# The first projection's data brought k-tile by k-tile, x and weights in one transfer

## The chip, the cores and the metric

The kernel runs on one core of a Trainium2 chip. The metric is device time in microseconds, the median of several runs of the whole program.

## The reference

Three transformer layers on one sequence of 256 tokens with 1024 features, in float32. The change is at the very start of the first, which has two attentions side by side:

```python
proj = jnp.einsum('bsd,df->bsf', h, w_in)          # 1024 -> 1440
c_q, c_kv, k_r, q_s, k_s, v_s = _split_cols(proj, AB_SPLITS)
q = jnp.einsum('bsr,rf->bsf', _rms_norm(c_q, q_norm), w_uq)
kv = jnp.einsum('bsr,rf->bsf', _rms_norm(c_kv, kv_norm), w_ukv)
o_a = _mla_attention(q_nope, q_rope, kv[..., :MLA_NOPE], k_rope, kv[..., MLA_NOPE:])
o_b = _swa_sink_attention(q_s, k_s, v_s, sinks)     # 8 heads, window of chunks
x = _layer_norm(ALPHA * x + concat(o_a, o_b) @ w_out); x = _layer_norm(ALPHA * x + swiglu(x))
```

A second layer with two other attentions and a third block with gates, a spatial mixer and cross-attention follow. The first stage below computes 512 of the 1440 columns: `c_q` (384) and `v_s` (128).

## The kernel before

**Exact products in three passes.** Each float32 operand is split into a high part, rounded to the type fp32r on ACT (a copy), and a low part, the rest, subtracted on DVE. A product is then x high times w high, x high times w low, x low times w high (`gx`, lines 421 to 428), all accumulated in one PSUM bank. In `gx` x (128 tokens) is the stationary side and the weights are the moving side, 512 columns wide in the first stage.

**Weights** come from one packed stream in HBM in the order in which the kernel asks for them (`raw`, `block`, `w`, lines 383 to 415). `block` issues a transfer on SP's queue, the high part on ACT and the low part on DVE. Later weights go through five buffers with the tag `raw`; in the first stage they land in buffers with the tag `h`.

**The first stage** (`start`, line 608). Seven products of a zeroed tile run first. Then x transposed and the 512 columns of weights come in five groups of k-tiles (a k-tile is 128 of the 1024 features): 0, 1, 2-3, 4-5, 6-7, each as one transfer of weights and one of x. `mixer_ab` (lines 674 to 677) forms 48 products: eight k-tiles, two token halves (`p1`, two PSUM banks), three passes. Then the values are copied out and the sum of squares of `c_q` is formed (lines 683 to 686), and the next stage (288 columns, lines 688 to 691), the norms and their transposes (`norm_T`), the other projections and the eight heads of each attention follow.

**What sets the order.** All instructions are recorded by the class `Order` and put in order by a planner (`issue`, lines 191 to 336): a list scheduler that replays each engine with assumed costs, latencies and a transfer rate (lines 46 to 54) and takes, on each engine, the ready instruction that was written first. So a change at the start also changes the planned times of what follows, and with them the order on every engine, until the planned order falls back into the old one. All instructions are emitted on line 336, which is why the profile shows L336 for nearly everything; tiles tell them apart: `g` are PSUM banks of projections, `a` those of attention and transposes, `h` split operands, `L` softmax tiles, `s` small ones, `xT` the split x.

Of the kernel before, what the change touches and what calls it, by code (L numbers as in the profile page):

```python
# [10 lines left out]
F32 = mybir.dt.float32  # L11
F32R = mybir.dt.float32r
AF = mybir.ActivationFunctionType
OP = mybir.AluOpType
# [3 lines left out]
S = 256  # L18
KT = D // 128
# [18 lines left out]
def ar(a, n):  # L38
    return list(range(a, a + n))
# [299 lines left out]
class Net:  # L339
# [268 lines left out]
    def start(self):  # L608
        nc, one = self.nc, self.one
        T = lambda name, shape: one(shape, F32, name)  # L610
        xt, self.xT = self.new_xT()
        self.xt0 = xt
        self.w_first = []
        rows = self.kt(KT)
        cols = ar(0, 384) + ar(1312, 128)
        z = self.tmpp([128, 128], F32, tag="si")
        nc.vector.memset(z, 0.0)
        p = self.pa()
        for i in range(WARM):
            nc.tensor.matmul(p[:, 0:128], z, z, start=True, stop=True)  # L620
        w = []
        for k0, k1 in ((0, 1), (1, 2), (2, 4), (4, 6), (6, 8)):
            w += self.w("ab_w_in", 0, rows[k0:k1], cols, self.hp)
            self.block(("xT", 0, rows[k0:k1], None), k1 - k0, S, out=(xt[:, 0, k0:k1, :], xt[:, 1, k0:k1, :]), pool=self.hp)
        self.g1 = w
        self.ident = T("ident", [128, 128])
        nc.sync.dma_start(self.ident, self.a["ident"], early=True)
        self.mhalf = T("mhalf", [128, 1])
        nc.gpsimd.memset(self.mhalf, -0.5)
        self.res = T("res", [128, 2, D])  # L630
# [38 lines left out]
    def mixer_ab(self):  # L669
        nc, V, A = self.nc, self.nc.vector, self.nc.scalar  # L670
        a, xT = self.a, self.xT
        rows = self.kt(KT)

        p1 = [self.pg(), self.pg()]
        for k in range(KT):
            for t in range(2):
                self.gx(p1[t], self.tok(xT[k:k + 1], t), self.g1[k:k + 1], k == 0, k == KT - 1)
        gq = self.gbp([128, 640], F32, tag="gb")
        self.bcast("ab_q_norm", 384, tile_=gq[:, 0:384])
        self.bcast("ab_kv_norm", 256, tile_=gq[:, 384:640])  # L680
# [7 lines left out]
        w = self.w("ab_w_in", 0, rows, ar(384, 288))  # L688
# [15 lines left out]
        w = self.w("ab_w_in", 0, rows, ar(1184, 128))  # L704
# [4 lines left out]
        for j in (0, 2):  # L709
            w = self.w("ab_w_in", 0, rows, [c for i in (j, j + 1) for hh in (i, 4 + i) for c in ar(672 + 64 * hh, 64)])  # L710
# [23 lines left out]
        for h0, nh in ((0, 5), (5, 3)):  # L734
            w = self.w("ab_w_uq", 0, self.kt(3), ar(h0 * 96, nh * 96))
# [8 lines left out]
        for j in (0, 1):  # L744
            w = self.w("ab_w_ukv", 0, self.kt(2), [c for hh in range(4 * j, 4 * j + 4) for c in ar(hh * 128, 64)])
# [17 lines left out]
        w = self.w("ab_w_ukv", 0, self.kt(2), [c for hh in range(8) for c in ar(hh * 128 + 64, 64)])  # L763
# [537 lines left out]
def pack(inputs, specs):  # L1301
    parts = []
    for name, li, rows, cols in specs:
        r = np.asarray(rows)
        if name == "xT":
            blk = inputs["x"][0].T[r.reshape(-1)]
        elif name == "memT":
            blk = inputs["mem_2"][0].T[r.reshape(-1)]
        elif name == "ffn":
            c = slice(cols * 128, cols * 128 + 128)  # L1310
            blk = np.concatenate([inputs["ffn_w_gate"][li][r.reshape(-1), c], inputs["ffn_w_up"][li][r.reshape(-1), c]], 1)
        else:
            blk = inputs[name][li][r.reshape(-1)]
            if len(cols) != blk.shape[1] or cols[0]:
                blk = blk[:, np.asarray(cols)]
        blk = blk.reshape(len(rows), 128, -1).transpose(1, 0, 2)
        parts.append(np.ascontiguousarray(blk).reshape(-1))
    return np.concatenate(parts)
# [27 lines left out]
```

## Time and profile before

| | us |
|---|---|
| median of 3 runs (929.24 to 930.12) | 929.69 |
| the profiled execution, whole | 929.24 |
| its span | 927.5 |
| PE busy | 916.5 (99%) |
| DVE busy | 600.4 (65%) |
| ACT busy | 484.1 (52%) |
| 16 transfer engines, queue of SP | 54.6% of the span |

The span is divided by engine: PE is TensorE's products, PEld its weight loads, DVE is VectorE, ACT is ScalarE, SP issues transfers. A busy PE counts from a product's start to its modelled end, so steps between starts say more than busy shares. In brackets behind a row stands the idle time of the engine before it and what ended it.

### The profile page before, as it was taken

Reading aid. Unit: us, or ns where it says so; the run is one execution under the profiler, and the core shown is the slowest. Engines: PE = TensorE matmul, PEld = TensorE weight load, DVE = VectorE, ACT = ScalarE, POOL = GpSimd, SP = SyncE. Lnnn points to the kernel's source line nnn. Section 1 sums busy time; section 2 is a strip of 40 time slices with the busy share of each in tenths; the row PEclk is TensorE's granted clock in tenths of the full one; section 3 lists DMA queues with packets and bytes.
Section 4 is the critical chain, followed back from the end, with each engine's and each line's share of the span. In section 5 each row is a group of like instructions: output and inputs, shape, how many; then the busy total and the mean of one; then the engine's idle time right before and its main releaser. Section 6 shows DMA issues by size and latency. Waiting matters only on the chain.

```text
span 927.5 us, 16281 instructions
## 1 busy us (share of the span) xinstructions
PE 916.5 (99%) x6504; PEld 846.4 (91%) x6504; DVE 600.4 (65%) x1064; ACT 484.1 (52%) x839; POOL 29.1 (3%) x40
## 2 busy tenths in 40 slices
PE   9999999999999999999999999999999999999997
PEld 7977999999888999789999988888889999999996
DVE  6798955555548588986455474685458697556553
ACT  6687544444434687745434463355456564444432
POOL 2100100000001000010000000100010010000000
PEclk9999999999999999999999999999999999999999
DMA  9754465456664754437555686175544546555631
GB/s 328 281 187 152 142 238 169 159 164 215 218 200 158 263 160 162 158 120 260 168 159 182 227 287 212 66 256 183 173 161 137 181 148 199 182 190 187 194 115 46
DMA packets 50157, 171.30 MB, mean 185 GB/s; under 512 B 5921, under 2 KB 7457, under 8 KB 49825
## 3 DMA queue, kind: packets, MB, share of 16 engines
q1 hardware_dynamic: 49792, 169.74, 54.6%
q8 instruction: 51, 0.84, 0.3%
q10 hardware_dynamic: 288, 0.52, 0.2%
q14 instruction: 26, 0.21, 0.1%
HBM read 169.19 MB, written 1.05 MB: 184 GB/s over the span
## 4 chain that ended last, share of the span: by engine, by line
PE 95%; ACT 2%; DVE 2%; DMA 1%; issue 0%; SPq 0%; POOL 0%; POOLq 0%; ACTq 0%
PE g L336 87%; PE a L336 8%; ACT h L336 1%; DVE h L336 1%; DMA h<-in_wstream_dram 1%; DVE L L336 0%; ACT L L336 0%; SPq L336 0%; ACT pt L336 0%; POOL s L336 0%; DVE s L336 0%; ACT y L336 0%; POOLq L1340 0%; ACT xT L336 0%; DVE res L336 0%
## 5 line engine op out<-in xcount | busy, mean ns | idle before, releaser
L336 DVE TENSOR_TENSOR h<-raw,h 128x1024 fp32r<-128x1024 f32 (+4 forms) x300 | 349.8, 1184 | 138.0 <-ACT h L336 108.4
L336 PE MATMUL g<-h,h 128*128 128x256 f32 (+2 forms) x2520 | 438.1, 330 | 0.0
L336 PEld LDWEIGHTS g<-h,h 128*128 128x128 f32 x2520 | 372.5, 188 | 44.7 <-issue 1.0
L336 ACT ACTIVATE h<-raw 128x1024 fp32r<-128x1024 f32 (+4 forms) x300 | 300.6, 1025 | 129.9 <-PE g L336 98.6
L336 PE MATMUL g<-xT,h 128*128 128x256 f32 x2424 | 295.3, 282 | 0.0
L336 PEld LDWEIGHTS g<-xT,h 128*128 128x128 f32 x2424 | 289.6, 188 | 0.9 <-issue 0.9
L336 PE MATMUL g<-h,xT 128*128 128x256 f32 (+3 forms) x744 | 112.4, 311 | 0.4 <-ACT xT L336 0.3
L336 PEld LDWEIGHTS g<-h,xT 128*128 128x128 f32 x744 | 102.1, 190 | 9.6 <-ACT xT L336 1.1
L336 ACT ACTIVATE si<-g 128x256 f32<-128x256 f32 x68 | 26.0, 382 | 125.9 <-PE g L336 124.0
L336 ACT ACTIVATE h<-g 64x512 fp32r<-64x512 f32 (+11 forms) x67 | 31.2, 474 | 52.0 <-PE g L336 38.3
L336 DVE TENSOR_TENSOR si<-si,g 128x256 f32<-128x256 f32 x50 | 21.0, 419 | 56.5 <-ACT si L336 56.0
L336 POOL TENSOR_TENSOR s<-s,mhalf 128x1 f32<-128x1 f32 x18 | 20.9, 1159 | 730.1 <-DVE s L336 730.1
L336 ACT ACTIVATE L<-L,s 128x128 f32<-128x128 f32 (+1 forms) x84 | 37.6, 450 | 10.6 <-DVE s L336 10.2
L336 DVE TENSOR_TENSOR h<-si,h 128x256 fp32r<-128x256 f32 x48 | 20.4, 425 | 16.3 <-ACT h L336 16.2
L336 PE MATMUL a<-ident,L 128*128 128x128 f32 (+1 forms) x132 | 25.9, 276 | 1.7 <-ACT h L336 1.3
L336 ACT ACTIVATE h<-si 128x256 fp32r<-128x256 f32 x48 | 19.7, 410 | 12.1 <-DVE si L336 12.0
L336 ACT ACTIVATE h<-a 128x256 fp32r<-128x256 f32 (+5 forms) x41 | 18.3, 474 | 14.7 <-PE a L336 14.3
L336 ACT ACTIVATE pt<-a 128x384 f32<-128x384 f32 (+1 forms) x42 | 20.7, 499 | 7.5 <-PE a L336 7.0
L336 DVE SCALAR_TENSOR_TENSOR res<-res,g 128x512 f32<-128x512 f32 x16 | 10.9, 683 | 20.5 <-PE g L336 20.5
L336 DVE TENSOR_SCALAR L<-L,s 128x128 f32<-128x128 f32 (+1 forms) x84 | 23.4, 321 | 1.1
L336 PE MATMUL a<-h,h 128*128 128x256 f32 (+5 forms) x152 | 23.0, 307 | 1.0 <-DVE h L336 0.7
L336 PE MATMUL a<-pt,h 128*64 128x256 f32 (+3 forms) x168 | 23.2, 332 | 0.0
(108 smaller groups left out, 437.1 us busy)
## 6 DMA issues: line engine op xcount, KB each, us to landing
raw<-in_wstream_dram SPq DMA_DIRECT2D x262, 512.0 KB, 4.1
raw<-in_wstream_dram SPq DMA_DIRECT2D x16, 384.0 KB, 3.0
raw<-in_wstream_dram SPq DMA_DIRECT2D x8, 516.0 KB, 4.4
raw<-in_wstream_dram SPq DMA_DIRECT2D x10, 256.0 KB, 2.8
gb<-in_ln_g_dram SPq DMA_DIRECT2D x4, 512.0 KB, 5.7
gb<-in_ln_b_dram SPq DMA_DIRECT2D x4, 512.0 KB, 6.5
h<-in_wstream_dram SPq DMA_DIRECT2D x3, 512.0 KB, 5.9
B<-in_swa_bias_dram SPq DMA_DIRECT2D x1, 1536.0 KB, 9.0
```

The costliest lines, as they stand in the source:

```text
L336: getattr(real, m)(*a, **k)
```

## The change

x and the weights of one k-tile come together: one transfer of 128 x 768 (256 columns of x, 512 of weights) for k-tiles 1 to 7, and for k-tile 0 still two, now x first. ACT splits x first, then w; for k-tile 0 the high part of w is half a copy on DVE and half one on ACT. High and low part of w lie in one tile. DVE subtracts for w and x of each k-tile. The 48 products are written pass by pass, both token halves in each pass. The packed stream gets a layout for the joint transfers.

```diff
-        for k0, k1 in ((0, 1), (1, 2), (2, 4), (4, 6), (6, 8)):
-            w += self.w("ab_w_in", 0, rows[k0:k1], cols, self.hp)
-            self.block(("xT", 0, rows[k0:k1], None), k1 - k0, S, out=(xt[:, 0, k0:k1, :], xt[:, 1, k0:k1, :]), pool=self.hp)
+        for k in range(KT):
+            hl = self.h([128, 2, 512], F32R)
+            if k == 0:
+                rx = self.raw(("xT", 0, rows[:1], None), 1, S, self.hp)[:, 0]
+                rw = self.raw(("ab_w_in", 0, rows[:1], cols), 1, 512, self.hp)[:, 0]
+            else:
+                r = self.raw(("xw", 0, rows[k:k + 1], cols), 1, S + 512, self.hp)[:, 0]
+                rx, rw = r[:, 0:S], r[:, S:]
+            nc.scalar.activation(xt[:, 0, k, :], rx, AF.Copy)
+            if k == 0:
+                nc.vector.tensor_copy(hl[:, 0, 0:256], rw[:, 0:256])
+                nc.scalar.activation(hl[:, 0, 256:512], rw[:, 256:512], AF.Copy)
+            else:
+                nc.scalar.activation(hl[:, 0], rw, AF.Copy)
+            nc.vector.tensor_tensor(hl[:, 1], rw, hl[:, 0].bitcast(F32), op=OP.subtract)
+            nc.vector.tensor_tensor(xt[:, 1, k, :], rx, xt[:, 0, k, :].bitcast(F32), op=OP.subtract)
+            w.append((hl[:, 0], hl[:, 1]))
...
         for k in range(KT):
-            for t in range(2):
-                self.gx(p1[t], self.tok(xT[k:k + 1], t), self.g1[k:k + 1], k == 0, k == KT - 1)
+            x, (wh, wl) = [self.tok(xT[k:k + 1], t)[0] for t in range(2)], self.g1[k]
+            for i, (hl, w) in enumerate(((0, wh), (0, wl), (1, wh))):
+                for t in range(2):
+                    nc.tensor.matmul(p1[t], x[t][hl], w, start=k == 0 and i == 0, stop=k == KT - 1 and i == 2)
...
+        elif name == "xw":
+            blk = np.concatenate([inputs["x"][0].T[r.reshape(-1)], inputs["ab_w_in"][li][r.reshape(-1)][:, np.asarray(cols)]], 1)
```

The order that results, at three places. First TensorE in the first stage, k-tiles 2 and 3 before (`g_110` and `g_111` are the two token halves, `h_96` holds the high parts of both k-tiles' weights, `h_97` the low parts; in brackets what the row waits for):

```order
L336 MATMUL g_110<-h_96,xT_84 128x512 [waits Activation_49]
L336 MATMUL g_111<-h_96,xT_84 128x512
L336 MATMUL g_110<-h_97,xT_84 128x512 [waits DVE_49]
L336 MATMUL g_111<-h_97,xT_84 128x512
L336 MATMUL g_110<-h_96,xT_84 128x512 [waits DVE_49]
L336 MATMUL g_111<-h_96,xT_84 128x512
L336 MATMUL g_110<-h_96,xT_84 128x512
```

And k-tile 2 now (`g_107` and `g_108` are the halves, `h_92` holds high and low part of its weights):

```order
L336 MATMUL g_107<-h_92,xT_84 128x512 [waits Activation_49]
L336 MATMUL g_108<-h_92,xT_84 128x512
L336 MATMUL g_107<-h_92,xT_84 128x512 [waits DVE_49]
L336 MATMUL g_108<-h_92,xT_84 128x512
...
L336 MATMUL g_107<-h_94,xT_84 128x512 [waits Activation_49]
L336 MATMUL g_108<-h_94,xT_84 128x512
```

Before, the products of two k-tiles wait for the splits of both; now each k-tile has its own tile and its own waits, and the halves alternate throughout (the two rows of the third pass read like those above and are left out).

Second TensorE in the projections after the first stage, at the transposes of the normed latent (`a_152` and `a_153` for the two token halves, from `h_143`). Before:

```order
L336 MATMUL g_157<-xT_84,h_156 128x256
L336 MATMUL a_152<-ident_107,h_143 128x128 x2
L336 MATMUL g_157<-xT_84,h_155 128x256 x2
...
L336 MATMUL g_165<-xT_84,h_160 128x256
L336 MATMUL g_165<-xT_84,h_161 128x256
L336 MATMUL g_165<-xT_84,h_160 128x256
L336 MATMUL a_153<-ident_107,h_143 128x128 x2
L336 MATMUL g_165<-xT_84,h_160 128x256
```

Now, with all numbers after the first stage lower by three:

```order
L336 MATMUL g_154<-xT_84,h_153 128x256
L336 MATMUL a_149<-ident_104,h_140 128x128 x2
L336 MATMUL g_154<-xT_84,h_152 128x256
L336 MATMUL g_162<-xT_84,h_157 128x256
L336 MATMUL g_162<-xT_84,h_158 128x256
L336 MATMUL g_162<-xT_84,h_157 128x256 x2
...
L336 MATMUL a_150<-ident_104,h_140 128x128 x2
L336 MATMUL g_162<-xT_84,h_157 128x256
```

The first pair stood before the last ten products of the `g_157` bank and stands before the last one of its counterpart `g_154`; the second stood behind three products of the next bank and stands behind eleven.

Third VectorE in the second attention (the ISA rows add the mask and take the maximum, the TENSOR_SCALAR rows scale the probabilities). Before, ahead of its first softmax and in it:

```order
L336 TENSOR_TENSOR h_368<-raw_366,h_367 128x1024
L336 TENSOR_TENSOR h_371<-raw_369,h_370 128x1024
L336 TENSOR_TENSOR h_374<-raw_372,h_373 128x1024
L336 ISA L_291,s_292<-a_289,mask_287 128x128
...
L336 RECIPROCAL s_294<-s_293 128x2
L336 TENSOR_SCALAR L_291<-L_291,s_294 128x128
L336 TENSOR_SCALAR L_291<-L_291,s_294 128x256
L336 ISA L_306,s_307<-a_304,mask_287 128x128
```

Now, in the middle of it:

```order
L336 RECIPROCAL s_306<-s_305 128x2
L336 TENSOR_SCALAR L_303<-L_303,s_306 128x128
L336 TENSOR_SCALAR L_303<-L_303,s_306 128x256
L336 TENSOR_TENSOR h_356<-raw_354,h_355 128x1024
L336 TENSOR_TENSOR h_285<-a_300,h_285 128x256
L336 RECIPROCAL s_312<-s_311 128x2
L336 TENSOR_SCALAR L_309<-L_309,s_312 128x128
```

The weight splits of the out-projection (`raw_357` and later before, `raw_354` and later now) stood within the first attention and ahead of the second, and now stand, from `h_356` on, between the second attention's softmax steps.

## Rows read from the trace of the kernel before

**Rows 1.** Page, parts 1 and 4: busy us and share; chain by engine.

```profile
PE 916.5 (99%) x6504; PEld 846.4 (91%) x6504; DVE 600.4 (65%) x1064; ACT 484.1 (52%) x839; POOL 29.1 (3%) x40
PE 95%; ACT 2%; DVE 2%; DMA 1%; issue 0%; SPq 0%; POOL 0%; POOLq 0%; ACTq 0%
```

**Rows 2.** Timeline, first stage, ACT and DVE: start, us, engine, operation [idle before].

```profile
3.52 0.63 ACT L336 ACTIVATE h<-h 128x512 fp32r<-128x512 f32 x1 [1.44 <-DMA h<-in_wstream_dram]
4.06 0.40 ACT L336 ACTIVATE xT<-h 128x256 fp32r<-128x256 f32 x1
4.18 0.69 DVE L336 TENSOR_TENSOR h<-h,h 128x512 fp32r<-128x512 f32 x1 [3.12 <-ACT h L336]
...
5.24 0.63 ACT L336 ACTIVATE h<-h 128x512 fp32r<-128x512 f32 x1 [0.79 <-DMA h<-in_wstream_dram]
...
6.27 0.42 ACT L336 ACTIVATE xT<-h 128x256 fp32r<-128x256 f32 x1 [0.40 <-DMA h<-in_wstream_dram]
...
7.55 1.06 ACT L336 ACTIVATE h<-h 128x1024 fp32r<-128x1024 f32 x1 [0.87 <-DMA h<-in_wstream_dram]
...
11.44 1.06 ACT L336 ACTIVATE h<-h 128x1024 fp32r<-128x1024 f32 x1 [0.39 <-DMA h<-in_wstream_dram]
```

**Rows 3.** PE, first stage: by tile; timeline; a stretch (last three: clock, DMA, GB/s).

```profile
L336 PE MATMUL g<-h,xT x48: 389/396/797, 4.5 to 17.8; 128*128 128x512 f32 x48
...
4.51 0.80 PE L336 MATMUL g<-h,xT 128*128 128x512 f32 x1
...
5.53 1.05 PE L336 MATMUL g<-h,xT 128*128 128x512 f32 x2
5.96 1.05 PE L336 MATMUL g<-h,xT 128*128 128x512 f32 x2
...
8.46 0.40 PE L336 MATMUL g<-h,xT 128*128 128x512 f32 x1
9.18 0.51 PE L336 MATMUL g<-h,xT 128*128 128x512 f32 x1 [0.33 <-ACT xT L336]
...
12.03 0.85 PE L336 MATMUL g<-h,xT 128*128 128x512 f32 x3
...
17.61 0.89 PE L336 MATMUL g<-h,xT 128*128 128x512 f32 x4
...
4.00:6.00 2.00, 1.96 (x7) 1.37 (x6) 1.12 (x3) 1.09 (x3) 1.55 (x3) 1.00 0.91 248
```

**Rows 4.** Timeline, PEld: weight loads of the norm's transposes.

```profile
26.89 0.20 PEld L336 LDWEIGHTS a<-ident,h 128*128 128x128 f32 x2 [0.18 <-DVE s L336]
...
29.00 0.20 PEld L336 LDWEIGHTS a<-ident,h 128*128 128x128 f32 x2 [0.35 <-DVE h L336]
```

**Rows 5.** Timeline, ACT after the first stage; a stretch: us, PE busy (count), others.

```profile
17.57 0.28 ACT L336 ACTIVATE h<-g 128x128 f32<-128x128 f32 x1 [1.55 <-PE g L336]
...
18.91 2.01 ACT L336 ACTIVATE h<-raw 128x1024 fp32r<-128x1024 f32 x2
...
20.00:22.00 2.00, 2.00 (x17) 2.00 (x16) 2.00 (x3) 1.39 (x3) 0.00 (x0) 1.00 0.97 393
```

**Rows 6.** First attention: PE, DVE; stretches (PE, PEld, DVE, ACT, POOL busy).

```profile
42.70 1.22 DVE L336 TENSOR_TENSOR h<-raw,h 128x1024 fp32r<-128x1024 f32 x1
...
55.31 0.55 PE L336 MATMUL a<-ident,L 128*128 128x128 f32 x3 [1.32 <-ACT h L336]
56.21 0.55 PE L336 MATMUL a<-ident,L 128*128 128x128 f32 x3 [0.36 <-DVE h L336]
56.69 1.55 PE L336 MATMUL a<-pt,h 128*64 128x256 f32 x8
...
62.18 0.87 PE L336 MATMUL a<-pt,h 128*64 128x256 f32 x8
...
50.00:55.00 5.00, 3.99 (x35) 3.08 (x33) 4.34 (x18) 4.72 (x16) 0.00 (x0) 1.00 0.76 308
...
75.00:80.00 5.00, 5.00 (x37) 3.94 (x35) 4.40 (x21) 4.87 (x18) 0.00 (x0) 1.00 0.01 3
```

## The prediction

> **What bounds the kernel now.** I read the busy shares and the chain first [rows 1]. PE is busy 99% of the span and has 95% of the chain, so a change can only give back time in which PE stands still or waits inside its stream. The first stage has such time, and I then read its splits on ACT and DVE [rows 2] and its products' starts [rows 3].
>
> What releases ACT's splits is DMA: the first weights are taken up at 3.52, those of k-tile 1 at 5.24, its x only at 6.27, the weights of k-tiles 2 and 3 (512 KB) at 7.55, those of k-tiles 6 and 7 at 11.44 [rows 2]. From 7.55 to 11.44 four k-tiles of 384 KB come, 0.97 us each: the pace of the transfers.
>
> The 48 products start between 4.51 and 17.8 [rows 3]. Early starts lie 0.43 us apart (5.53, 5.96), later ones 0.2325 (24 products from 12.03 to 17.61). 512 columns in 0.43 us are the 1.2 GHz level, 0.2325 is near 2.4 GHz, though the granted-clock column reads 1.00 throughout (4 to 6 us). Between the 4th start (5.96) and the 12th (8.46) lie 8 steps in 2.50 us: 3 slow, 5 fast, so the clock rises near 7.3, after PE was busy with warm-up and products since 1.1 us.
>
> Now the loss. The 12th product starts at 8.46, so the 13th could at 8.69; it starts at 9.18 and waits for x of k-tiles 2 and 3: 0.49 us. From there to the 48th are 35 steps in 8.62 us; at 0.2325 they take 8.14: 0.48 lost in small waits for the other splits of those two k-tiles. **0.97 us** in all.
>
> **The change, part by part.** *Transfers.* Ten become nine with the same 3 MB, so the pace of 0.97 us per k-tile stays. Against it PE needs six products per k-tile: 1.40 us at the full clock, 2.6 at half. ACT's splits of one k-tile cost 0.40 + 0.63 = 1.03 [rows 2]; DVE's subtraction costs 0.69 for 512 columns and at most that for 256, so at most 1.4, by ACT's ratio (0.40 to 0.63) nearer 1.13. All three are at or below PE's need. So once PE has started, no k-tile after the second should be waited for, and the 0.97 us goes.
>
> *Start.* x lands before w, and w's first split is halved between ACT and a copy on DVE. No row shows that copy; its bounds are nothing beyond what ACT does beside it and DVE's 0.69 for twice the columns; I take ACT's 0.40 for the half. Both data of k-tile 0 were there by 4.06 [rows 2]; with splits of 0.40 beside each other PE starts at 4.2 to 4.6, where it was 4.51. I take 4.35: 0.15 us at the low clock, worth 0.1. DVE has x's subtraction queued ahead of its copy, which is why it is not more; the queue behind is the weight's subtraction, wanted only by the third product.
>
> *k-tile 1.* Its x and w now land together: no earlier than 0.97 after k-tile 0 (about 5.0) and no later than 6.27, where x is taken up today although more data stood in the queue beside it. Plus 1.03 on ACT that is 6.0 to 7.3; PE ends k-tile 0 at about 4.35 + 6 × 0.43 = 6.95. The wait is 0 to 0.35, I take 0, since the middle is 6.65.
>
> The page "DMA: Bandwidth & Descriptors" of the Trainium skill, section "Why a DMA increments its semaphore by 16 and not by 1", says that only the full count tells that all of a transfer has landed. By that rule a merged transfer makes x wait for the last piece of w, against this change; the trace agrees as far as w and x of k-tile 1, two transfers today, are taken up a microsecond apart. By the rule's worst case the wait is the 0.35 above; by the pace in the rows it is nothing.
>
> *Pass order.* The products go over both token halves in each pass, where before the order changed from k-tile to k-tile. Count and width stay (48 of 512), so it costs nothing by itself. It ends both halves together. Before, half 0 was done three products before the end and ACT took it up at 17.57 [rows 5]. Now the third weight split of the next stage (576 columns) stands on ACT behind three evictions that wait for the end of the stage, where before it stood ahead of them. With the stage ending about 17.0, the evictions (1.34 us from 17.57 to 18.91 before, with a fourth) and the split (at most the 1.0 of a wider one at 18.91) end by 19.0, DVE's part by 20. The cover is 20 products of 288 columns, 17 in a 2 us slice: 2.4 to 2.6 us, so it is wanted at about 19.5. Covered on ACT, tight on DVE; if the cover is gone, 0.5.
>
> *Transposes at 27 and 29 us.* Before, the weight loads of two pairs of transposes wait 0.18 and 0.35 [rows 4], because the latent's norm was not ready. In the new order the pairs stand nine and eight products later. A product of 256 columns is half of the 0.2325, so 0.9 to 1.0 us of more cover. I take 0.35 gained, bounds 0 and 0.53.
>
> *The order in the attentions.* The planner also rearranges everything up to about 120 us. What matters is DVE. Before, two weight splits of 1.22 us stand among the first attention's softmaxes, and one just ahead, as at 42.70 [rows 6]; PE there waits 1.32 at 55.31, 0.36 at 56.21, and needs 1.55 instead of 0.87 for the value products at 56.69: 2.36 us lost. Now they stand later, and three splits stand among the second attention's softmaxes, where before none did and PE did not wait. DVE is nearly full in both stretches (4.34 of 5 us at 50 to 55, 4.40 of 5 at 75 to 80), so time moved out of one is moved into the other. Bounds: all 2.36 gained and nothing lost; or nothing gained and three splits fully exposed, 3 × 1.22 = 3.66 lost. I take 0, between the two and nearer to the row of the first.
>
> Late in the chain the order is the old one and PE is full, so what is gained by 120 us should stand at the end.
>
> **Sum.** −0.97 − 0.1 − 0.35 + 0 = −1.4 us. The profiled execution took 929.24 (span 927.5 and 1.74 around it), so its counterpart takes 927.8; the median of the three runs is 929.69, 0.45 above the profiled one, and the forecast for a median is **928.3**. A measurement of this kernel tells about 0.2% from no change, 1.86 us: the line lies at 927.83, just below the forecast.
>
> **Rivals.**
>
> *The attentions gain as well.* With the splits out of the way the first attention's 2.36 us of waits shrink and the second's pipeline holds. For it: the waits are behind DVE, and DVE loses 3.66 us of work there. Against it: the second attention's softmaxes are now served two at a time where PE had issued the scores of several pairs ahead. Gain 1.2 to 2.36 more: about 926.4.
>
> *k-tile 1 late and the clock with it.* If it is ready at 7.3, PE pauses 0.35 just where its clock rose before. The page "TensorE: Matmul & The Clock Gate" of the Trainium skill, section "What's actually happening", says that the default is throttled and sustained activity releases it. The trace agrees that products run at half pace before they run at full. In rows: a product at the low level costs 0.2 more, so a rise one k-tile later costs 6 × 0.2 = 1.2, and the first stage's gain is used up: 928.3 + 1.2 = about 929.5, no change. Against it: the transfers' pace has k-tile 1 in time. That the change does not do what it says, PE still waiting for each k-tile, ends at the same figure.
>
> *Splits ahead of softmaxes (the other side).* In the second attention a 1.22 us split stands on DVE between two halves of a pair's softmax; the next transposes wait for it, PE has fewer scores issued ahead and runs dry. Three splits fully exposed cost 3.66, less 1.4: 2.2 slower, about 931.9. It decides from 1.4 us of exposed waits on. For it: DVE's load. Against it: the out-projection's first products stand between as filler, and the last gains of the first attention would have to fail too.
>
> **How the numbers follow.** Forecast 0.51 (927.3 to 929.2; 0.20 of it under the 0.2% line); attentions gain 0.20; late k-tile 0.18; slower 0.11 (0.09 of it beyond 0.2%). Faster 0.20 + 0.20 = 0.40; same 0.31 + 0.18 + 0.02 = 0.51; slower 0.09. The range, 926.3 to 930.3, takes in the forecast and the late k-tile, most of the attentions' gain and the nearest part of the slower case; outside are the last tenth below and the fully exposed splits above.
>
> **What the new profile would show.** Right: products 13 to 48 at 0.23 us steps without a gap, the stage's last start near 16.8 instead of 17.8, both weight loads of the transposes at 26 to 29 us without a wait, PE's waits between 50 and 85 us about 2.4 us as before but in other places. Wrong: a gap at k-tile 1 near 7 us, half pace after 7.5, a wait for the third weight split near 19.5, or waits for DVE in 60 to 85 us that exceed those gone before 60.

## The result, and the profile after

The changed kernel takes 925.38 us (median of 6 runs, 924.75 to 925.78), the kernel before 929.9 beside it: a ratio of 0.9942 (95% interval 0.9931 to 0.9953). Forecast were 928.3 with a range of 926.3 to 930.3. The gain is 4.5 us by the medians and 5.4 by the ratio, three to four times the forecast 1.4, and the time lies below the range.

The profiled execution takes 924.75 with a span of 923.0, so 4.5 us of span went. Part 1 and part 4 of its page (busy us and share by engine; the chain by engine):

```profile
PE 913.9 (99%) x6504; PEld 845.5 (92%) x6504; DVE 602.0 (65%) x1071; ACT 485.3 (53%) x845; POOL 28.3 (3%) x40
PE 93%; DVE 3%; ACT 2%; DMA 1%; issue 1%; POOL 0%; POOLq 0%; SPq 0%; ACTq 0%
```

Beside [rows 1] they tell little: the shares of DVE and ACT, 65% and 53%, are nearly what they were. The stretches tell. Two starts cut the program in three: that of the first stage's 48th product (worked out from the starts of the single products) and that of the fourth pair's value products in the first attention (the last such row of [rows 6]; 58.15 below).

| us | before | after | difference |
|---|---|---|---|
| start to the 48th product | 17.84 | 16.58 | -1.26 |
| 48th product to the fourth pair's value products | 44.34 | 41.57 | -2.77 |
| from there to the start of the program's last product | 858.42 | 858.18 | -0.24 |
| behind it | 6.9 | 6.7 | -0.2 |

So over half of the gain lies in the middle piece, where the change edited nothing: there only the order of issue is new. (The trace of the kernel before has the earliest 48th product of the five traces with the old stage, see below; beside their median the stage gives more than 1.26.)

The first stage on ACT and DVE (start, us, engine, operation, idle before it), which answers to [rows 2]:

```profile
2.85 0.42 ACT L336 ACTIVATE xT<-h 128x256 fp32r<-128x256 f32 x1 [0.77 <-DMA h<-in_wstream_dram]
4.21 0.42 ACT L336 ACTIVATE h<-h 128x256 fp32r<-128x256 f32 x1 [0.94 <-DMA h<-in_wstream_dram]
4.21 0.47 DVE L336 CAST h<-h 128x256 fp32r<-128x256 f32 x1 [0.48 <-DMA h<-in_wstream_dram]
...
5.19 0.42 ACT L336 ACTIVATE xT<-h 128x256 fp32r<-128x256 f32 x1 [0.57 <-DMA h<-in_wstream_dram]
5.51 0.61 ACT L336 ACTIVATE h<-h 128x512 fp32r<-128x512 f32 x1
...
8.19 0.42 ACT L336 ACTIVATE xT<-h 128x256 fp32r<-128x256 f32 x1 [1.10 <-DMA h<-in_wstream_dram]
8.52 0.62 ACT L336 ACTIVATE h<-h 128x512 fp32r<-128x512 f32 x1
9.12 0.42 ACT L336 ACTIVATE xT<-h 128x256 fp32r<-128x256 f32 x1
```

and on PE, with the stretch of [rows 3] (last three columns: clock, DMA share, GB/s):

```profile
4.82 13.35 PE L336 MATMUL g<-h,xT 128*128 128x512 f32 x57 [0.35 <-DVE h L336]
4.00:6.00 2.00, 1.65 (x6) 1.14 (x5) 1.53 (x3) 1.23 (x3) 1.59 (x3) 1.00 1.08 355
```

The last data of k-tile 0 are taken up at 4.21 (4.06 before) and the first product starts 0.31 later than before. But then one row runs on through the stage without a wait: from the fifth product (6.63) to the 48th (16.58) the steps are 0.23 throughout. ACT's splits of k-tile 1 are done at 6.1, in time. ACT waits 1.10 for k-tile 3 (8.19) without PE running out of products, and from there on it works off one k-tile after another with hardly a wait for DMA.

Behind the stage, the two pairs of transposes on PEld, the third weight split on ACT (with the evictions ahead of it) and DVE, and the stretch of [rows 5]:

```profile
26.45 0.24 PEld L336 LDWEIGHTS a<-ident,h 128*128 128x128 f32 x2
28.10 0.25 PEld L336 LDWEIGHTS a<-ident,h 128*128 128x128 f32 x2
```

```profile
16.78 0.51 ACT L336 ACTIVATE h<-g 128x128 f32<-128x128 f32 x2 [1.44 <-PE g L336]
17.19 0.49 ACT L336 ACTIVATE y<-g 128x384 f32<-128x384 f32 x1
...
17.65 0.69 ACT L336 ACTIVATE h<-raw 128x576 fp32r<-128x576 f32 x1
18.37 0.76 DVE L336 TENSOR_TENSOR h<-raw,h 128x576 fp32r<-128x576 f32 x1 [0.42 <-ACT h L336]
20.00:22.00 2.00, 2.00 (x18) 2.00 (x17) 2.00 (x4) 1.43 (x3) 0.00 (x0) 1.00 1.11 371
```

The waits of [rows 4] are gone, and PE is full (2.00 of 2.00) where the third split might have been missed. Then the first attention on PE, which answers to [rows 6]: `pt,h` are value products, `ident,L` the transposes of a pair's probabilities, `h,h` other products that fill in; at the end the two stretches.

```profile
50.03 0.87 PE L336 MATMUL a<-pt,h 128*64 128x256 f32 x8
50.83 0.55 PE L336 MATMUL a<-ident,L 128*128 128x128 f32 x3
51.13 1.04 PE L336 MATMUL g<-h,h 128*128 128x288 f32 x6
...
52.49 0.52 PE L336 MATMUL g<-h,h 128*128 128x288 f32 x2
...
53.15 1.02 PE L336 MATMUL a<-pt,h 128*64 128x256 f32 x8
...
58.15 0.87 PE L336 MATMUL a<-pt,h 128*64 128x256 f32 x8
50.00:55.00 5.00, 4.91 (x40) 3.75 (x38) 4.76 (x25) 4.63 (x20) 0.00 (x0) 1.00 0.01 4
75.00:80.00 5.00, 5.00 (x34) 3.32 (x33) 4.18 (x10) 4.75 (x11) 0.00 (x0) 1.00 0.35 116
```

PE is busy 4.91 of 5 us at 50 to 55, where it was 3.99. Eight products of 288 columns now stand between the second pair's value products (50.03) and the third's (53.15). Before, all products of that kind had gone by when the second pair's value products came at 53.12, and nothing was left to do until 55.31. The chain of waits of the kernel before, in order of time (start, us, what), says what PE was then waiting behind:

```profile
52.12 0.23 PE a L336 x2
...
52.37 1.22 DVE h L336
...
53.62 0.17 DVE s L336
```

The timeline has its 1.22 us piece on DVE by name, PE's last work ahead of the wait, and what ACT did meanwhile:

```profile
52.37 1.22 DVE L336 COPY h<-a 32x1024 f32<-32x1024 f32 x1 [0.49 <-PE a L336]
53.12 0.87 PE L336 MATMUL a<-pt,h 128*64 128x256 f32 x8
...
54.24 1.42 ACT L336 ACTIVATE h<-a 32x1024 f32<-32x1024 f32 x2
```

The piece on DVE is not a weight split but a copy of 32 x 1024 (the transposed rope key, out of PSUM), and the softmaxes of two heads queue behind it. The 1.32 us of [rows 6] are put down to ACT: ACT has a 32 x 1024 copy of its own there, which ends at 55.26, and DVE's second softmax ends at 55.43; so the rope key holds up both. In the new order DVE's copy stands behind all softmaxes of the first attention (58.95), and so do the three weight splits that stood just ahead of and among them. I shall call these splits and copies the helper work.

### The profile page after: what moved, and what is told of

It reads as the page before. It is cut to its first block, busy times and chain, and to the rows that moved or that the text cites. A ratio compares the mean times of both kernels' runs of the same rounds, so it can differ in the third digit from the quotient of the medians.

```text
span 923.0 us, 16287 instructions
## 1 busy us (share of the span) xinstructions
PE 913.9 (99%) x6504; PEld 845.5 (92%) x6504; DVE 602.0 (65%) x1071; ACT 485.3 (53%) x845; POOL 28.3 (3%) x40
## 4 chain that ended last, share of the span: by engine, by line
PE 93%; DVE 3%; ACT 2%; DMA 1%; issue 1%; POOL 0%; POOLq 0%; SPq 0%; ACTq 0%
PE g L336 85%; PE a L336 8%; DVE h L336 2%; ACT h L336 1%; DMA raw<-in_wstream_dram 1%; DVE res L336 0%; POOL s L336 0%; DMA h<-in_wstream_dram 0%; DVE s L336 0%; DVE L L336 0%; DVE xT L336 0%; ACT L L336 0%; ACT pt L336 0%; POOLq L1358 0%; ACT y L336 0%
## 5 line engine op out<-in xcount | busy, mean ns | idle before, releaser
L336 ACT ACTIVATE h<-g 64x512 fp32r<-64x512 f32 (+10 forms) x67 | 31.3, 475 | 52.3 <-PE g L336 38.6
```

Source lines behind the costliest of these rows:

```text
L336: getattr(real, m)(*a, **k)
```

## The experiments

In all of them a table fixes the order of issue behind the first stage; a kernel with the new stage and the table of the changed kernel has its order on every engine. A is the start of the 48th product, B that of the fourth pair's value products, C that of the last product, so B-A and C-B are the ways between them; all are of one profiled execution of each kernel. The ratio is to the kernel before, run beside it on the same chip, with its 95% interval. Beside the experiments the kernel before took 930.2 to 930.8, not 929.9, so kernels are better compared by their ratios than by their medians; the recorded expectations were reckoned from 929.9 and 925.4.

| kernel | median us | ratio | A | B-A | C-B |
|---|---|---|---|---|---|
| before | 929.9 | 1 | 17.84 | 44.34 | 858.4 |
| after | 925.38 | 0.9942 (0.9931 to 0.9953) | 16.58 | 41.57 | 858.2 |
| old stage, new order | 928.01 | 0.9972 (0.9963 to 0.9981) | 18.20 | 41.57 | 859.6 |
| new stage, old order | 928.61 | 0.9987 (0.9978 to 0.9996) | 16.88 | 45.35 | 858.8 |
| before, copies late | 929.77 | 0.9993 (0.9985 to 1.0002) | 18.49 | 43.81 | 859.0 |
| before, DVE's splits late | 931.82 | 1.0015 (1.0006 to 1.0024) | 18.45 | 44.23 | 860.0 |
| before, all helpers late | 934.32 | 1.0034 (1.0022 to 1.0046) | 18.47 | 45.41 | 860.8 |
| after, splits early | 930.07 | 0.9991 (0.9982 to 1.0000) | 16.27 | 46.03 | 858.4 |
| after, copies early | 928.23 | 0.9979 (0.9968 to 0.9990) | 16.35 | 44.83 | 858.5 |
| after, all helpers early | 933.05 | 1.0023 (1.0012 to 1.0034) | 18.51 | 48.21 | 858.8 |
| after, x and w apart | 926.27 | 0.9951 (0.9939 to 0.9963) | 16.19 | 41.63 | 859.4 |
| after, half by half | 926.30 | 0.9961 (0.9948 to 0.9974) | 16.53 | 41.54 | 859.6 |
| after, coarse grain | 927.66 | 0.9969 (0.9958 to 0.9981) | 18.40 | 41.51 | 858.7 |
| old stage x first, new order | 927.57 | 0.9968 (0.9955 to 0.9980) | 18.54 | 41.47 | 859.6 |
| after, w first | 926.15 | 0.9950 (0.9937 to 0.9963) | 16.99 | 41.53 | 858.7 |
| after, one more warm-up | 926.39 | 0.9956 (0.9943 to 0.9968) | 17.55 | 41.55 | 859.2 |

Eight kernels with the new order have a B-A of 41.47 to 41.63, whatever their first stage does; for that order it is a sharp instrument. In the old order it is not: the kernel before and "new stage, old order" have one order and differ by 1.0 (44.34 and 45.35). C-B differs among the eight by up to 1.5 us, so nothing under that is put down to a cause there.

**The stage and the order apart.** The old first stage with the new order behind it, and the other way round:

```diff
 # old stage, new order: the kernel before, and
+        seq = [first stage as planned] + [the rest in the changed kernel's order]
 # new stage, old order: the changed kernel, and
+        seq = [first stage as planned] + [the rest in the order of the kernel before]
```

> The first stage is as in the kernel before (its transfers, splits and order of products); everything behind it is issued in the order of the changed kernel. Theory 'order': of the 4.3 us gained, the first stage itself gave 1.24 and the rest comes from the order behind it (0.55 at the transposes, about 1.95 in the two attentions, about 0.5 later), so this kernel gains about 2.5 to 3 us: 927.1 against 929.9. In its trace PE should wait for DVE nowhere between 50 and 60 us. Rival 'earlier start': the attentions ran dry because the weights for their fillers and their splits came too late against PE, and an earlier first stage is what mended it; then the order by itself gives at most the 0.55 of the transposes: about 929.4. Rival 'the order needs the new start': with half 1 of the first stage ending late the new order's own waits appear, a loss: 930.5 or more.

> The first stage is as in the changed kernel; everything behind it is issued in the order of the kernel before. Theory 'order': only the first stage's 1.24 us is gained, and the waits of 1.32 and 0.36 us in the first attention stand as before: about 928.6. Rival 'earlier start': all of the gain is here, about 925.5. Rival 'DVE copy' and rival 'weight splits' both agree with 'order' here.

The new order gives its 2.77 us with the old stage too, so it does not need the new one. By its ratio that kernel gains 2.6 us, as theory "order" forecast (2.5 to 3). Its C-B is 1.2 over that of the kernel before; 0.35 of that is a wait of PE at 119.18 for DVE and ACT, where ACT had stood for a weight transfer until 116.47; the rest is not assigned. The second kernel gains 1.2 us by its ratio, as "order" had it, and not the whole gain: "earlier start" has fallen. In its trace PE waits as before (1.32 and 0.35 us), and its clock then falls (last three columns: clock, DMA share, GB/s):

```profile
54.31 0.55 PE L408 MATMUL a<-ident,L 128*128 128x128 f32 x3 [1.32 <-ACT h L408]
55.21 0.55 PE L408 MATMUL a<-ident,L 128*128 128x128 f32 x3 [0.35 <-DVE h L408]
55.69 2.23 PE L408 MATMUL a<-pt,h 128*64 128x256 f32 x8
57.85 1.41 PE L408 MATMUL g<-h,h 128*128 128x256 f32 x5
55.00:56.00 1.00, 0.79 (x4) 0.60 (x5) 1.00 (x6) 0.80 (x3) 0.00 (x0) 0.84 0.99 400
56.00:57.00 1.00, 1.00 (x6) 0.60 (x5) 0.96 (x6) 1.00 (x4) 0.00 (x0) 0.50 0.46 176
58.00:59.00 1.00, 1.00 (x5) 1.00 (x6) 0.84 (x4) 0.82 (x3) 0.00 (x0) 0.50 0.00 0
```

The same value products took 1.55 before [rows 6], the five products behind them 0.86: in this trace the stage's gain is lost again to a clock at 0.50, the lower level, for some three microseconds.

**Helper work late, in the old order.** Moved behind the softmaxes of the first attention: the copies (with PE's two transposes for them); DVE's halves of two weight splits; or all helper work at once. With the splits go the transfers that reuse their buffers.

```diff
 # DVE, kernel before, copies late
-COPY h<-a 32x1024            ahead of the third pair's softmax
+COPY h<-a 32x1024            behind the fourth pair's softmax
 # DVE, splits late
-TENSOR_TENSOR h<-raw,h 128x1024   two, among the softmaxes
+TENSOR_TENSOR h<-raw,h 128x1024   two, behind the fourth pair's softmax
```

> The kernel before, with one thing moved: the two transposes of the rope key, its 32 x 1024 copy on DVE and the one on ACT are issued behind the softmaxes of all four heads of the first attention, as in the changed kernel; the two weight splits stay among the softmaxes. Theory 'DVE copy': PE waited 1.32 and 0.36 us because this 1.22 us copy stood on DVE ahead of two softmaxes; these waits go, 1.2 to 2.2 us gained: about 928.0, and no wait of PE for DVE over 0.3 us at 50 to 58 us. Theory 'weight splits' (that of the prediction): nothing gained, 929.9, since the two splits of 1.22 us still stand there.

> The kernel before, with the other thing moved: the two weight splits of 1.22 us on DVE that stand among the softmaxes of the first attention (and the two transfers that reuse their raw buffers) are issued behind the softmaxes of all four heads; the 32 x 1024 copies stay where they were. Theory 'weight splits': 1.5 to 2.4 us gained, 927.5 to 928.4. Theory 'DVE copy': little gained, since the copy still stands ahead of two softmaxes; 0 to 0.5 us, 929.4 to 929.9, and PE's wait for DVE near 55 us stands, perhaps shorter. If both matter alike, each of the two kernels gains about half.

> The kernel before with its old first stage and its own order of PE's work and of the softmaxes; moved behind the softmaxes of the first attention are both kinds of helper work at once: the 32 x 1024 copies on DVE and ACT, and three weight splits of 1024 columns with both their halves (and the three transfers that reuse their raw buffers). Theory 'load': the two waits of PE in the first attention go, and by the value products of the fourth pair (before: 56.2 to 58.2 us) PE is 1.5 to 2.4 us earlier than in the kernel before, as in the kernel with the whole new order (2.1). What comes behind is crowded with the same work and the later transfers, so up to 1.5 us may be given back by 75 us: total 928 to 930. Rival 'PE's order': the helper work is not what matters, PE's own fillers stand in better places in the new order; then the gain at the fourth pair is the 0.8 of the copies alone.

The copies alone: the third pair's value products come 37.92 us after A instead of 38.85, so 0.93 gained (the new order has them at 36.57); by the fourth pair 0.53 is left, and the total cannot be told from no change. The DVE splits alone: 0.1, and 1.6 us lost behind (C-B). All together: 37.93 for the third pair, no better than the copies alone, then 1.1 us worse than before by the fourth pair and 2.4 worse behind it; 934.3 in all, where 928 to 930 was forecast. Up to the third pair, then, moving all helper work gives 0.9 of the 2.3 us that the new order gains there, 0.55 of them at the transposes and 1.7 in the attention; the theory "load" has fallen as it stood. What PE waits for in the first and the third of these kernels, the first one's chain, and DVE in the third:

```profile
55.48 0.99 PE L408 MATMUL a<-ident,L 128*128 128x128 f32 x5 [0.68 <-ACT pt L408]
```

```profile
52.06 0.23 PE a L408 x2
...
52.31 0.49 ACT pt L408
52.80 0.49 ACT L L408 x2
53.29 0.18 ACT s L408
53.47 0.89 ACT L L408 x4
```

```profile
62.62 1.33 PE L408 MATMUL g<-h,h 128*128 128x256 f32 x9 [1.60 <-DVE L L408]
```

```profile
61.19 1.23 DVE L408 TENSOR_TENSOR h<-raw,h 128x1024 fp32r<-128x1024 f32 x1 [0.67 <-ACT h L408]
62.33 0.23 DVE L408 TENSOR_TENSOR L<-g,rope 128x80 f32<-128x80 f32 x1
```

With the copy gone, the chain goes over ACT: the third pair's exponentials (from 52.80) stand behind the eviction of the second pair's transposes, and these transposes come only at 52.06, because PE has other products ahead of and among them. So PE's order holds the softmaxes back too. The 1.60 us in the third kernel are of its own making: a moved split (61.19) stands ahead of the rope steps (62.33) that PE's products wait for, which is so neither before the change nor in the new order. Less those 1.60 its B-A would be 43.8, that of the copies alone (an estimate, by subtraction); what it does behind the third pair says nothing of the place that the new order gives the helper work.

**Helper work early, in the new order.** The opposite: the helper work is put back among the softmaxes, the rest of the new order is kept. It does not get back to its old places exactly. PE's order is left alone, and in it the copy's two transposes come ahead of the third pair's value products (52.84 after the change), not of the second's (51.95 before), so DVE's copy stands behind the reciprocals of six of the eight heads, where before the change it stood behind those of four; and DVE's third split stands behind those of four, where it stood behind two.

```diff
 # ACT and DVE, changed kernel, splits early
+ACTIVATE h<-raw 128x1024, TENSOR_TENSOR h<-raw,h 128x1024   one pair ahead of, two among the softmaxes
 # copies early
+COPY h<-a 32x1024 (DVE), ACTIVATE h<-a 32x1024 (ACT)        ahead of the fourth pair's softmax
```

> The changed kernel with one thing put back: three weight splits of 1024 columns, the ACT halves and the DVE halves (1.0 and 1.22 us each), stand where the kernel before has them, one pair just ahead of and two among the first attention's softmaxes; the 32 x 1024 copies stay behind the softmaxes. Theory 'load': what cost the first attention about 2 us was all of the helper work among its softmaxes on ACT and DVE together (three splits and one copy on each), and the splits are three quarters of it; then this loses 1 to 2 us against the changed kernel, PE waits again near 52 to 57 us for ACT or DVE, about 926.5 to 927.5. Theory 'DVE copy' alone: no loss, 925.4. Rival 'clock': if PE stands still for over a microsecond here, the granted clock may fall as it did with the new first stage under the old order (0.50 for 3 us), and the loss is 2 to 3 us.

> The changed kernel with the other thing put back: the rope key's two transposes, its 32 x 1024 copy on DVE and the one on ACT stand where the kernel before has them, ahead of the last softmaxes of the first attention; the weight splits stay behind. Theory 'load': one quarter of the helper work, with slack left by the absent splits: 0 to 0.8 us lost, 925.4 to 926.2. Theory 'DVE copy': 1.2 to 2 us lost, 926.6 to 927.4, with a wait of PE for DVE over 0.8 us near 50 us.

> The changed kernel with both kinds of helper work put back to where the kernel before has them: the three weight splits (4.4 us lost alone) and the copies (3.1 us lost alone, of which about 1.4 is the clock that fell). Theory 'load': the same work as before the change now stands among the softmaxes, but PE's order is that of the changed kernel, which has less other work between the pairs, so the loss is larger than the 2 us gained by moving it: 5 to 7.5 us against the changed kernel, 930.5 to 933. Rival 'the pieces overlap': no more than the larger of the two alone, about 4.4: 930.

B-A grows by 4.46 with the splits, 3.26 with the copies, 6.64 with both, all more than the 2.77 that the whole new order gains, and the first two more than any theory had priced. For the splits the chain goes over DVE and ACT from 42 to 56 us, with splits in it on both (first fence); in the second kernel it is the copy, with PE's waits and the clock (second fence):

```profile
49.62 1.28 ACT h L408 x2
...
50.92 1.22 DVE h L408
```

```profile
53.01 1.22 DVE L408 COPY h<-a 32x1024 f32<-32x1024 f32 x1 [0.38 <-PE a L408]
55.32 0.73 PE L408 MATMUL g<-h,h 128*128 128x256 f32 x4 [1.39 <-DVE L L408]
56.37 0.30 PE L408 MATMUL a<-ident,L 128*128 128x128 f32 x1 [0.31 <-DVE L L408]
58.00:60.00 2.00, 2.00 (x11) 1.97 (x11) 1.97 (x12) 0.05 (x2) 0.00 (x0) 0.50 0.00 0
```

Of the copies' 3.26 us, 1.70 are the two waits; the remaining 1.56 fall where the clock is at 0.50. In the kernel with both the clock stays at 1.00 (56 to 66 us), and there the splits' 4.46 and the copies' 1.70 nearly add up (6.2 against 6.6), as "load" had it. So helper work among the softmaxes costs PE's new order several microseconds; what it cost in its old places these kernels do not tell.

**What the first stage's gain is made of.** One part undone at a time, in the changed kernel, and one part done alone in the old stage:

```diff
 # x and w apart
-                r = self.raw(("xw", 0, rows[k:k + 1], cols), 1, S + 512, self.hp)[:, 0]
+            rx = self.raw(("xT", 0, rows[k:k + 1], None), 1, S, self.hp)[:, 0]
+            rw = self.raw(("ab_w_in", 0, rows[k:k + 1], cols), 1, 512, self.hp)[:, 0]
 # half by half
-            for i, (hl, w) in enumerate(((0, wh), (0, wl), (1, wh))):
-                for t in range(2):
+            for t in range(2):
+                for i, (hl, w) in enumerate(((0, wh), (0, wl), (1, wh))):
 # coarse grain
-        for k in range(KT):
+        for k0, k1 in ((0, 1), (1, 2), (2, 4), (4, 6), (6, 8)):
 # old stage, x first
+            if k0 == 0: x's transfer and split ahead of the weights'
```

> The changed kernel with x and the weights of every k-tile in two transfers, x first, instead of one (16 transfers in place of 9; the same bytes, splits and order of products). If the merged transfer is what keeps the first stage's products fed, the splits of some k-tile are taken up later here and PE gets a gap: the stage ends 0.3 us or more later. If the grain (one k-tile at a time) and the split on landing do it, the stage ends within 0.2 us of the changed kernel's 16.8. Issue of the extra seven transfers on SP (0.47 us each) comes ahead of later loads: up to 3.3 us later there, hidden as long as the next stage's weights are not waited for. I expect no more than 0.3 us of difference in the total.

> The changed kernel with the first stage's products issued token half by token half inside a k-tile (three of half 0, then three of half 1), as in every second k-tile before the change, instead of pass by pass. Theory 'order of products does nothing': same count and width, so the stage ends as in the changed kernel (four profiles of that first stage so far have its last product start between 16.3 and 16.9 us) and the total is the same, 925.4 to 926.2. Rival 'pass order feeds PE': half by half the second product already needs the weight's low part, so the start of k-tile 0 gets a gap of about 0.4 us, and the stage ends that much later.

> The changed kernel with k-tiles 2 to 7 in pairs again (x and weights of a pair in a transfer each, split as a pair), k-tiles 0 and 1 as changed. Theory 'grain': the stall at the third k-tile comes back, because a pair's splits cost 1.06 + 0.62 us on ACT after the landing of 768 KB where a single k-tile's cost 1.03; the stage's last product starts 0.5 to 1.0 us later than in the changed kernel, at 17.0 to 17.6. Rival 'early landing': x ahead of the weights brought k-tile 1's data a microsecond earlier (taken up at 5.2 to 5.5 us in all traces with x first, complete at 6.1 to 6.6 in all with the weights first) and that is the gain; then this ends within 0.2 us of the changed kernel.

> The first stage of the kernel before, with one thing changed: k-tile 0's x is transferred and split ahead of its weights; behind the stage the order of the changed kernel. Against the same kernel with the weights first (last product of the stage at 18.2, total 928.0). Theory 'early landing': k-tile 1 is complete about a microsecond earlier, and the stage ends 0.3 to 1.0 us earlier. Theory 'grain': the stage is held by the pairs from k-tile 2 on, so it ends within 0.3 us of 18.2.

Of the three parts only the grain shows: with pairs, A is 18.40, later than the 17.0 to 17.6 forecast and as in the old stage (17.84 to 18.49 in its five traces); with x and w apart 16.19 and half by half 16.53, as in the changed kernel's stage (16.27 to 16.88 in four traces; a fifth is told of at the end). By the medians of five traces each, 18.45 and 16.58, the stage gives 1.9 us. These are single traces: in the total the coarse kernel is 1.4 us behind "half by half" by the medians, but the intervals of their ratios overlap. And the pairs are both landed and split together there, so which of the two stalls PE was not told apart. The coarse kernel's stalls stand at its 13th and 15th product:

```profile
9.38 0.73 PE L408 MATMUL g<-h,xT 128*128 128x512 f32 x2 [0.96 <-ACT h L408]
10.64 8.55 PE L408 MATMUL g<-h,xT 128*128 128x512 f32 x37 [0.53 <-DVE h L408]
```

In the old stage with x first, k-tile 1 did come earlier (its x is split at 5.98 instead of 6.27 to 6.64), and the stage ended no earlier for it (18.54).

**Two tries at more.**

```diff
 # w first: k-tile 0's weights ahead of x, x's split shared too
+                nc.scalar.activation(xt[:, 0, 0, 0:128], rx[:, 0:128], AF.Copy)
+                nc.vector.tensor_copy(xt[:, 0, 0, 128:256], rx[:, 128:256])
 # one more warm-up
-WARM = 7
+WARM = 8
```

> The changed kernel, with k-tile 0's weights transferred ahead of its x, and x's first split shared between ACT (token half 0) and DVE (token half 1) too. In the changed kernel the last of the two lands at 4.21 us and the products start at 4.82, 0.3 later than before the change (4.51). With x last, two splits of 128 columns instead of 256 follow the landing: start at 4.4 to 4.55, 0.3 to 0.4 us earlier at the low clock. If the clock rises as much earlier, the stage ends 0.3 us earlier: about 925.1. If the following k-tiles' data set the pace, the stage's end does not move: 925.4.

> The changed kernel with eight warm-up products instead of seven, so that PE is busy up to about 4.6 us and does not stand still for 0.35 us before the first product at 4.82. In the one trace in which PE went from the warm-up to the products without standing still and k-tile 0 was there at 4.3, products ran at full pace from 5.2 us on; in the others, with the pause, from 5.7 to 6.6. If the pause delays the clock, full pace comes before 5.7 here and the stage ends 0.2 to 0.4 us earlier: about 925.1. If not, nothing changes: 925.4.

With w first the products start at 4.31, the best of all, but k-tile 1 is complete only at 6.12 and PE stands still for 0.85 us at its first product: nothing gained. With one more warm-up product k-tile 0's weights came late in the profiled run (4.95), so PE paused for 0.81 us all the same; it decides nothing. Neither beats the changed kernel.

## Why the prediction was wrong, point by point

*The failed step* is "The order in the attentions", with its sentence "time moved out of one is moved into the other" and its value of 0. The middle piece gained 2.77: 0.55 at the transposes and 2.2 in the first attention; the second attention gives back 0.3. So the term was -1.9, not 0. Three things were wrong in that step. I blamed the weight splits, though the chain at 52.37 leads to the copy; I had read the rows of the waits and not what stood ahead of them. I took a DVE at 4.34 and 4.40 of 5 us for one that can take no more; but the second attention took up the splits and PE stayed at 5.00 of 5. And I left PE's own order out: eight filling products moved to where the softmax is waited for, and the transposes ahead of them. That the order of issue gains the time, with either first stage, is shown (B-A 41.57 twice). How it divides is shown only up to the third pair: there the helper work moved late gives 0.9 in the old order of PE, and the whole new order 1.7 besides the 0.55 of the transposes. That PE's own order makes the rest is argued from the chain and the filling products, not shown, since no kernel has PE's new order with the helper work in exactly its old places, or the reverse. The gain is the first rival, at 0.20; its price of 1.2 to 2.36 was right, its reason was not: with two of DVE's splits out of the way 0.1 was gained by the fourth pair.

*Start*: 4.82, not 4.35. The halves of the split cost 0.42 and 0.47, nearly the 0.40 assumed, but w, now second, was taken up at 4.21 and the first product came 0.14 after the splits. A loss of 0.31 where 0.1 was counted as gained.

*k-tile 1*: in time, as forecast; the rival of a late k-tile did not come about in the changed kernel, though k-tile 1 was late with w first (0.85).

*Stalls of the first stage*: 0.97 was counted (1.0 with the 48th start at 17.84 instead of the rounded 17.8). From the 12th product to the 48th it now takes 8.32 us instead of 9.39, so 1.07 went; another 0.2 was gained up to the 12th in spite of the late start, because full pace began at 6.63 instead of 7.52. By the experiments the old stage's stall at the 13th product was small in the trace that I had (0.49); in others of its traces the step there is 1.3 to 1.7 us. The reason given, splits of one k-tile within PE's need, held as far as the grain was tested; "merged" and "pass by pass" show no effect.

*The third weight split*: it stands on ACT behind three evictions, as forecast; DVE's part ends at 19.1, nearly a microsecond earlier than allowed for, and is not waited for. *Transposes*: 0.55, at the upper bound of 0.53 and not at 0.35, since both pairs' waits went.

*The rest*: 0.24 us from the fourth pair to the last product, the second attention's loss included, and 0.2 behind it are within what kernels of one order differ by.

## What to carry to other kernels

Before pricing a wait, follow the chain from it to the instruction that stood ahead, and look at what the waiting engine could have done meanwhile; a busy share of nearly one on the helper engine tells neither. An order of several in-order queues is best tested whole: pieces put back cost 3.3 to 6.6 us where the whole gained 2.8, and pieces taken over alone gained at most 0.5. When data are split after landing and arrive no slower than they are used, look at the grain in which they land and are split before the number of transfers: here 16 transfers did as well as 9.

## What the runs showed of the hardware

The clock's rise in the first stage is not tied to the code alone. With the same first stage, products ran at full pace from 5.7 to 6.6 us in four traces, but in one, where the weights of k-tile 0 came 0.4 us later (pause of 0.93 before the first product), at half pace up to 10.17, and A was 18.51 with no stall at all:

```profile
5.39 13.78 PE L408 MATMUL g<-h,xT 128*128 128x512 f32 x50 [0.93 <-DVE h L408]
6.00:8.00 2.00, 2.00 (x6) 1.61 (x5) 1.34 (x4) 1.16 (x4) 0.00 (x0) 1.00 1.02 387
8.00:10.00 2.00, 2.00 (x6) 1.52 (x5) 1.90 (x5) 1.97 (x5) 0.00 (x0) 1.00 1.04 416
```

The single starts lie 0.43 us apart up to there, which is the lower level, though the clock column reads 1.00. The kernel with one more warm-up product paused for 0.81 us and had full pace from 6.48, so a pause of nearly a microsecond does not by itself decide it. Nor does a wait decide the fall: two waits of 1.32 and 0.36 us left the clock at 1.00 before the change (1.32 and 0.35 did so too with DVE's splits late), and 1.32 and 0.35 a microsecond earlier in the program took it to 0.50.

When k-tile 1 is complete went with which of the first two transfers goes first: it was taken up whole at 5.2 to 6.0 us in ten traces with x (128 KB) first, at 6.1 to 6.6 in six with the weights (256 KB) first. Where little else differed it was 5.98 against 6.27 to 6.64 (old stage) and 5.2 to 5.9 against 6.12 (new stage); x first in the old stage and the weights first in the new are one trace each. Why was not tried.
